# First norm of a hybrid decoder block: the order in which four blocks of rows are loaded, turned and evicted

## The chip, the cores and the metric

The kernel runs on one core of a Trainium2 chip. The core has TensorE (PE, the matrix unit, with its weight loads listed as PEld), VectorE (DVE), ScalarE (ACT), GpSimd (POOL) and SyncE (SP). SP, ACT and POOL can issue DMA transfers, each on a queue of its own. The metric is the device time of one execution in microseconds (us). The profile shows one execution; its span runs from the first to the last instruction.

## The reference

One layer over 512 tokens of width 2048, everything in float32: an RMS norm, one input projection to all branches, a gated short convolution beside a causal attention with a forget bias, a gated merge, an output projection, a second norm, and an MLP with a squared ReLU, then a last norm.

```python
def reference(x, g_mix, w_in, b_f, b_gate, conv_w, w_conv_out, w_attn_out,
              w_mix_out, g_mlp, w_ff1, w_ff2, g_final):
    b, s, _ = x.shape
    for l in range(DEPTH):
        h = rmsnorm(x, g_mix[l])
        z = jnp.einsum('bsd,dc->bsc', h, w_in[l])
        cb, cc, cv, q, k, v, f_logit, gate_c, gate_a = jnp.split(z, SPLIT_POINTS, axis=-1)
        conv_y = cb * causal_dwconv(cc * cv, conv_w[l])
        conv_branch = jnp.einsum('bsc,cd->bsd', conv_y, w_conv_out[l])
        log_f = jax.nn.log_sigmoid(f_logit.astype(jnp.float32) + b_f[l].astype(jnp.float32))
        attn = forgetting_attention(q.reshape(b, s, N_HEADS, HEAD_DIM),
                                    k.reshape(b, s, N_HEADS, HEAD_DIM),
                                    v.reshape(b, s, N_HEADS, HEAD_DIM), log_f)
        attn_branch = jnp.einsum('bsc,cd->bsd', attn, w_attn_out[l])
        gc = jax.nn.sigmoid(gate_c + b_gate[l, :D_MODEL])
        ga = jax.nn.sigmoid(gate_a + b_gate[l, D_MODEL:])
        merged = gc * conv_branch + ga * attn_branch
        x = x + jnp.einsum('bsd,de->bse', merged, w_mix_out[l])
        h = rmsnorm(x, g_mlp[l])
        u = jnp.square(jax.nn.relu(jnp.einsum('bsd,df->bsf', h, w_ff1[l])))
        x = x + jnp.einsum('bsf,fd->bsd', u, w_ff2[l])
    return rmsnorm(x, g_final)
```

What matters here is the beginning: `h = rmsnorm(x, g_mix)`, and the first products of `h` with columns of `w_in` (attention V, K and Q).

## The kernel before

The 512 tokens are four blocks of 128 rows. A block of `x` (128 x 2048, 1 MB) lies in SBUF with tokens on the partitions. The products need it the other way round, with features on the partitions, so the first norm does the following for each block (`Quarters.block`, line 354): four ScalarE squares with running sums (`square_part`, line 327), one small VectorE reduction and a GpSimd power for the reciprocal root (`rstd_of`, line 320), a diagonal matrix `dg` that holds that factor (line 358), then matmuls of the block against `dg` that turn and scale it at once into a PSUM bank, four tiles of 128 x 128 a bank, with banks 6 and 7 in turn (line 362). VectorE evicts each bank in two instructions that also multiply by the gain of the feature (line 367). The profile counts each of these turning matmuls as two records: 32 for a block.

Products are made by a seven-product scheme over 2 x 2 quarters. The activations are cut into token halves (blocks 0 and 1; blocks 2 and 3) and into even and odd tiles of features: quarters A11, A12 for the first token half, A21, A22 for the second, and four sums and differences S1 to S4 of them. Each float32 operand is split into a high part, rounded by a ScalarE copy (line 101), and a low part, which VectorE subtracts out (line 102); each product is then three matmuls, high by high, high by low, low by high. Quarters lie in SBUF as such pairs (`put`, line 351).

A group of columns (class `Group`, line 166) has two column halves of four weight quarters, 1 MB each, which `load` brings in on SP's queue (line 180), into one of four buffers x0 to x3 that a list `free` hands round. Its work is cut in two:

- `head` (line 216) loads two weight quarters, X[0, 0] and X[1, 0], multiplies them by A11 and A12 and adds the two results. It needs blocks 0 and 1 only. Each of the two products is 48 matmuls of 128 x 256; the weights' split goes into `th` and `tl`, two buffers of each.
- `tail` (line 232) makes the other five products with S4, S2, S3, S1 and A22, and needs all four blocks.

The first five groups are one of V (`gV0`, through `mm_rows`, where the first 24 matmuls of a product need only block 0 and the other 24 block 1) and four of K and Q (through `mm_cols`, each matmul needing both blocks). The code runs the five heads, then `Q1.sums()` (line 375: four VectorE sums or differences of 128 x 2048 and four splits), then the five tails.

The code before the heads loads the four blocks on SP's queue, block 0 in four pieces and the others in two (lines 390 to 395), the small rows of gains and biases on ScalarE's queue behind block 0 in the code (lines 397 to 406), then squares and turns block 0, block 1, and then squares of blocks 2 and 3 before both are turned. Blocks 0 and 1 are split into A11 and A12 as soon as each is turned, blocks 2 and 3 into A22 (lines 369 to 373). The rest of the kernel (attention, convolution, gates, merge, MLP) is not touched.

No order of instructions is written out by hand. The framework places each instruction in its engine's queue by its position in the code and by when it takes its inputs to be ready, and it adds the waits. An engine's queue is then worked through in that fixed order. So an instruction that stands later in the code can be queued earlier, and an instruction whose input is late holds up what is queued behind it.

Of the kernel before, what the change touches and what calls it, by code (L numbers as in the profile page):

```python
# [15 lines left out]
P = 128  # L16
# [29 lines left out]
def tile_hybrid_block(ctx: ExitStack, tc, x, g_mix, w_in, b_f, b_gate, conv_w, w_conv_out,  # L46
# [118 lines left out]

    class Group:
# [7 lines left out]
        def load(self, i, j):  # L174

            t = main.tile([P, KT // 2, self.w], F32, tag=f"x{free[0]}", name=f"x{i}{j}")
            self.at[i, j] = free.pop(0)
            c = self.cs[j]
            src = self.view[:, c:c + self.w].rearrange("(q two p) c -> two p q c", two=2, p=P)
            nc.sync.dma_start(out=t, in_=src[i])  # L180
            return t
# [34 lines left out]
        def head(self, keep=False, between=lambda: None):  # L216

            X = self.X = {}
            X[0, 0], X[1, 0] = self.load(0, 0), self.load(1, 0)
# [110 lines left out]
    class Quarters:  # L330
# [23 lines left out]
        def block(self, xt, part, t):  # L354
# [4 lines left out]
            for c in range(4):  # L359
# [6 lines left out]
                for par in range(2):  # L366
                    nc.vector.tensor_tensor(out=self.H[i, par][:, 2 * c:2 * c + 2, ts], in0=p2[:, par],
                                            in1=g2[:, par].unsqueeze(2).to_broadcast([P, 2, P]), op=ALU.mult)
# [3 lines left out]
            else:  # L372
                self.put("A22", self.H[1, 1], ts)
# [14 lines left out]
    xin = []  # L388
    xp = [pair(2 + i, F32, "xn") for i in range(2)]
    for t in range(NT):  # L390
        h = xp[t // 2][:, t % 2]
        n = 4 if t == 0 else 2
        for i in range(n):
            nc.sync.dma_start(out=h[:, i * D // n:(i + 1) * D // n], in_=x[t * P:(t + 1) * P, i * D // n:(i + 1) * D // n])
        xin.append(h)
        if t == 0:
            rows = main.tile([NV, P], F32, tag="x3", name="rows")
            r0 = 0
            for src, n in ((g_mix[0], KT), (g_mlp[0], KT), (b_gate[0], 2 * KT)):
                nc.scalar.dma_start(out=rows[r0:r0 + n, :], in_=src.rearrange("(k p) -> k p", p=P))  # L400
                r0 += n
            nc.scalar.dma_start(out=rows[r0:r0 + 3 * CT, :], in_=conv_w[0].rearrange("j (k p) -> (j k) p", p=P))
            nc.scalar.dma_start(out=bf, in_=b_f.to_broadcast([P, NH]))
            pv = bank(7, "pv")
            nc.tensor.transpose(pv[:, :NV], rows, ident[:NV, :NV])
            nc.vector.tensor_copy(cols, pv[:, :NV])
# [6 lines left out]
    def squares(t):  # L413
        for i in range(4):
            square_part(xin[t][:, i * S:(i + 1) * S], ss1[:, t, i:i + 1], junk[:, i * S:(i + 1) * S])

# [636 lines left out]
```

## Time and profile before

| | |
|---|---|
| median of 3 runs | 2546.12 us (2540.99 to 2546.52) |
| the profiled execution | 2549.66 us |
| its span | 2547.8 us |
| TensorE's mean granted clock | 0.992 |
| TensorE busy | 2469.5 us, 97% of the span |
| TensorE busy in the first 50 us | 37.27 us |
| VectorE busy, first 40 to 60 us and 60 to 80 us | 19.35 and 19.99 of 20 us |
| ScalarE busy in the same stretches | 13.09 and 11.73 of 20 us |
| GpSimd busy in the same stretches | 0.00 and 2.56 of 20 us |

How to read a row of the timelines: start, duration, engine, line of the kernel, operation, what it writes and what it reads, the tile's shape and number of instructions; in brackets how long the engine stood idle before it and what ended that wait. PE's busy time counts matmuls from start to modelled end, so neighbours overlap: what a product takes is read from the starts. A helper's line (101, 102, 105, 108) stands for all its uses, so tiles tell them apart: `xn` are rows of x, `ptr` the turned banks, `h` the evicted quarters, `A` and `S` the split quarters, `x` the weights, `th` and `tl` their split, `a` to `d` the accumulators. A row such as SPq or ACTq is an engine's queue issuing a DMA.

### The profile page before, as it was taken

How to read it: one execution, taken by the hardware profiler on the slowest of the kernel's cores; microseconds unless marked ns; L12 is line 12 of the kernel's file. 1: busy time of each engine (PE TensorE's matmuls, PEld its weight loads, DVE VectorE, ACT ScalarE, POOL GpSimd, SP SyncE). 2: the span in 40 equal slices, each digit the busy share in tenths (PEclk: the TensorE clock that was granted, in tenths of full speed). 3: DMA queues.
4: the chain of work that ended last, by engine and by line, in shares of the span. 5: the costliest groups of instructions: out<-in, count | busy, mean ns of one | idle time of the engine just before them, and what ended most of it. 6: DMA issues, size and time to landing. Idle time of an engine off the chain costs nothing.

```text
span 2547.8 us, 39010 instructions
## 1 busy us (share of the span) xinstructions
PE 2469.5 (97%) x16895; PEld 2269.4 (89%) x16895; DVE 1904.8 (75%) x1498; ACT 1144.5 (45%) x1120; POOL 128.2 (5%) x184
## 2 busy tenths in 40 slices
PE   8999999999999999999989999999999999999997
PEld 7999899999999988888889999999998887787785
DVE  7877677779767734435778888888887878878888
ACT  6433443344444622235545655655654333333343
POOL 0000000000000000000001111111111000000000
PEclk9999999999999999999999999999999999999998
DMA  7554444466443544436565665757587556654573
GB/s 240 158 186 153 155 137 129 133 195 210 138 150 115 199 159 143 136 118 231 167 199 182 216 218 189 246 171 236 193 299 286 181 210 219 226 194 162 191 256 106
DMA packets 287871, 473.45 MB, mean 186 GB/s; under 512 B 10236, under 2 KB 194644, under 8 KB 283476
## 3 DMA queue, kind: packets, MB, share of 16 engines
q1 hardware_dynamic: 260704, 330.40, 40.6%
q0 software_dynamic: 26128, 139.47, 14.7%
q8 instruction: 132, 2.16, 0.3%
q10 hardware_dynamic: 868, 1.10, 0.1%
q14 instruction: 39, 0.32, 0.0%
HBM read 374.46 MB, written 96.47 MB: 185 GB/s over the span
## 4 chain that ended last, share of the span: by engine, by line
PE 49%; DVE 12%; DMA 10%; issue 6%; ACT 4%; POOL 1%; POOLq 0%; ACTq 0%; SPq 0%; DVEq 0%
DMA s_d<-r 5%; DVE tl L102 5%; DMA x<-in_w_ff_dram 4%; ACT th L101 4%; PE a L137 3%; PE a L139 3%; PE a L141 3%; PE a L154 3%; PE a L155 2%; PE a L157 2%; PE pt L295 2%; PE pn L304 2%; PE pn L302 2%; PE pt L297 2%; PE pn L303 2%
## 5 line engine op out<-in xcount | busy, mean ns | idle before, releaser
L102 DVE TENSOR_TENSOR tl<-x,th 128x2048 fp32r<-128x2048 f32 (+1 forms) x252 | 576.0, 2289 | 215.0 <-ACT th L101 199.9
L101 ACT ACTIVATE th<-x 128x2048 fp32r<-128x2048 f32 (+1 forms) x252 | 481.8, 1916 | 474.1 <-PE a L139 164.2
L105 DVE TENSOR_TENSOR x<-x,x 128x2048 f32<-128x2048 f32 (+1 forms) x144 | 329.3, 2287 | 32.5 <-DMA x<-in_w_ff_dram 24.8
L101 ACT ACTIVATE th<-y 128x2048 fp32r<-128x2048 f32 x80 | 153.6, 1921 | 270.2 <-DVE y L105 102.9
L102 DVE TENSOR_TENSOR tl<-y,th 128x2048 fp32r<-128x2048 f32 x80 | 182.8, 2285 | 43.6 <-ACT th L101 43.6
L137 PE MATMUL a<-ST,th 128*128 128x256 f32 x768 | 186.1, 286 | 22.6 <-ACT th L101 19.7
L154 PE MATMUL a<-th,us 128*128 128x512 f32 x512 | 201.7, 394 | 4.4 <-ACT o L836 3.4
L102 DVE TENSOR_TENSOR tl<-raw,th 128x2048 fp32r<-128x2048 f32 x40 | 91.7, 2293 | 150.7 <-ACT th L101 150.2
L155 PE MATMUL a<-th,us 128*128 128x512 f32 x512 | 200.1, 391 | 0.0
L139 PE MATMUL a<-ST,th 128*128 128x256 f32 x768 | 184.4, 283 | 0.0
L137 PEld LDWEIGHTS a<-ST,th 128*128 128x128 f32 x768 | 149.7, 195 | 25.4 <-ACT th L101 22.3
L101 ACT ACTIVATE th<-raw 128x2048 fp32r<-128x2048 f32 x40 | 76.7, 1918 | 176.7 <-PE pt L296 71.5
L139 PEld LDWEIGHTS a<-ST,th 128*128 128x128 f32 x768 | 149.7, 195 | 0.0
L137 PE MATMUL a<-S,th 128*128 128x256 f32 x576 | 136.2, 280 | 4.3 <-ACT th L101 4.2
L157 PE MATMUL a<-tl,us 128*128 128x512 f32 x512 | 136.8, 389 | 0.1
L139 PE MATMUL a<-S,th 128*128 128x256 f32 x576 | 135.6, 279 | 0.0
L154 PEld LDWEIGHTS a<-th,us 128*128 128x128 f32 x512 | 96.6, 189 | 29.6 <-ACT th L101 6.2
L137 PE MATMUL d<-ST,th 128*128 128x256 f32 x512 | 118.1, 277 | 1.0 <-ACT o L194 1.0
L139 PE MATMUL d<-ST,th 128*128 128x256 f32 x512 | 118.0, 276 | 0.0
L155 PEld LDWEIGHTS a<-th,us 128*128 128x128 f32 x512 | 96.7, 189 | 19.7
L157 PEld LDWEIGHTS a<-tl,us 128*128 128x128 f32 x512 | 96.0, 188 | 20.4 <-DVE tl L102 0.5
L137 PEld LDWEIGHTS a<-S,th 128*128 128x128 f32 x576 | 108.5, 188 | 5.6 <-ACT th L101 5.3
(276 smaller groups left out, 6257.8 us busy)
## 6 DMA issues: line engine op xcount, KB each, us to landing
x<-in_w_in_dram SPq DMA_DIRECT2D x86, 1024.0 KB, 5.8
x<-in_w_ff_dram SPq DMA_DIRECT2D x66, 1024.0 KB, 8.4
y<-in_w_ff_dram SPq DMA_DIRECT2D x64, 1024.0 KB, 6.2
us<-s_d POOLq DMA_DIRECT2D x24, 2048.0 KB, 10.0
s_d<-rh POOLq DMA_DIRECT2D x32, 896.0 KB, 6.4
s_d<-r POOLq DMA_DIRECT2D x32, 896.0 KB, 7.8
raw<-in_w_mix_out_dram SPq DMA_DIRECT2D x24, 1024.0 KB, 5.1
g_d<-o SPq DMA_DIRECT2D x32, 256.0 KB, 2.2
```

What stands on the lines that cost most here:

```text
L101: nc.scalar.activation(out=hi, in_=src, func=AF.Copy)
L102: nc.vector.tensor_tensor(out=lo, in0=src, in1=hi.bitcast(F32), op=ALU.subtract)
L105: nc.vector.tensor_tensor(out=out, in0=a, in1=b, op=ALU.subtract)
L137: nc.tensor.matmul(o, hi[:, q, js], Sh, start=first and q == 0 and j == 0, stop=False, skip_group_check=True)
L139: nc.tensor.matmul(o, hi[:, q, js], Sl, start=False, stop=False, skip_group_check=True)
L141: nc.tensor.matmul(o, lo[:, q, js], Sh, start=False, stop=q == nq - 1, skip_group_check=True)
L154: nc.tensor.matmul(o, Sh, hi[:, q, :], start=begin and q == 0, stop=False, skip_group_check=True)
L155: nc.tensor.matmul(o, Sl, hi[:, q, :], start=False, stop=False, skip_group_check=True)
L157: nc.tensor.matmul(o, Sh, lo[:, q, :], start=False, stop=q == nq - 1, skip_group_check=True)
L295: nc.tensor.matmul(ps[j], hi[:, q, js], xh, start=k == 0, stop=False)
L297: nc.tensor.matmul(ps[j], lo[:, q, js], xh, start=False, stop=k == kt - 1)
L302: nc.tensor.matmul(ps, xh, hi, start=first, stop=False)
```

## The change

- A helper `behind(place, done)` has GpSimd copy one column of `done` into the place that a DMA will overwrite, so that this DMA comes after whatever wrote `done`.
- Block 0 comes in two halves on SP's queue and block 1 in two halves on ScalarE's, ahead of the small rows there. Blocks 2 and 3 each come in one DMA on GpSimd's queue, and only after `last_part`, the last column of block 1's low part of A12, is written.
- The first group's first weight load waits for the first element of block 0's evicted quarter, its second weight load for `last_part`.
- Blocks 0 and 1 are squared and turned at the start. Block 2 is squared and turned behind the first head in the code, block 3 behind the second.
- The banks of blocks 2 and 3 are evicted by ScalarE, 16 copies of 128 x 128 a block with the gain as a factor by partition, in place of VectorE's 8 of 128 x 256.
- A22 is split once as a whole (128 x 2048), in place of twice 128 x 1024.

```diff
@@ -163,6 +163,10 @@

     free, later = [0, 1, 2, 3], []

+    def behind(place, done):
+
+        nc.gpsimd.tensor_copy(place, done)
+
     class Group:

 
@@ -171,12 +175,14 @@
             self.view, self.cs, self.w, self.ST, self.mm, self.banks = view, (c1, c2), w, ST, mm, banks
             self.put, self.scale, self.at = put, scale, {}

-        def load(self, i, j):
+        def load(self, i, j, after=None):

             t = main.tile([P, KT // 2, self.w], F32, tag=f"x{free[0]}", name=f"x{i}{j}")
             self.at[i, j] = free.pop(0)
             c = self.cs[j]
             src = self.view[:, c:c + self.w].rearrange("(q two p) c -> two p q c", two=2, p=P)
+            if after is not None:
+                behind(t[:, 0, 0:1], after)
             nc.sync.dma_start(out=t, in_=src[i])
             return t

@@ -213,10 +219,10 @@
         def done(self, *ij):
             free.append(self.at.pop(ij))

-        def head(self, keep=False, between=lambda: None):
+        def head(self, keep=False, between=lambda: None, after=(None, None)):

             X = self.X = {}
-            X[0, 0], X[1, 0] = self.load(0, 0), self.load(1, 0)
+            X[0, 0], X[1, 0] = self.load(0, 0, after[0]), self.load(1, 0, after[1])
             self.a = self.acc("a")
             self.run(self.a, "A11", X[0, 0], True)
             s1 = self.snap(self.a)
@@ -364,13 +370,16 @@
                 p2 = pt.rearrange("p (q two b) -> p two q b", two=2, b=P)
                 g2 = self.gT[:, 4 * c:4 * c + 4].rearrange("p (q two) -> p two q", two=2)
                 for par in range(2):
-                    nc.vector.tensor_tensor(out=self.H[i, par][:, 2 * c:2 * c + 2, ts], in0=p2[:, par],
-                                            in1=g2[:, par].unsqueeze(2).to_broadcast([P, 2, P]), op=ALU.mult)
+                    if i == 0:
+                        nc.vector.tensor_tensor(out=self.H[i, par][:, 2 * c:2 * c + 2, ts], in0=p2[:, par],
+                                                in1=g2[:, par].unsqueeze(2).to_broadcast([P, 2, P]), op=ALU.mult)
+                        continue
+                    for q in range(2):
+                        nc.scalar.activation(out=self.H[i, par][:, 2 * c + q, ts], in_=p2[:, par, q], func=AF.Copy,
+                                             scale=g2[:, par, q:q + 1])
             if i == 0:
                 self.put("A11", self.H[0, 0], ts)
                 self.put("A12", self.H[0, 1], ts)
-            else:
-                self.put("A22", self.H[1, 1], ts)

         def sums(self):
             H = self.H
@@ -385,43 +394,39 @@

     ph = ExitStack()
     px = ph.enter_context(phase("px"))
-    xin = []
     xp = [pair(2 + i, F32, "xn") for i in range(2)]
-    for t in range(NT):
-        h = xp[t // 2][:, t % 2]
-        n = 4 if t == 0 else 2
+    xin = [xp[t // 2][:, t % 2] for t in range(NT)]
+
+    def load_x(t, n, queue=nc.sync):
         for i in range(n):
-            nc.sync.dma_start(out=h[:, i * D // n:(i + 1) * D // n], in_=x[t * P:(t + 1) * P, i * D // n:(i + 1) * D // n])
-        xin.append(h)
-        if t == 0:
-            rows = main.tile([NV, P], F32, tag="x3", name="rows")
-            r0 = 0
-            for src, n in ((g_mix[0], KT), (g_mlp[0], KT), (b_gate[0], 2 * KT)):
-                nc.scalar.dma_start(out=rows[r0:r0 + n, :], in_=src.rearrange("(k p) -> k p", p=P))
-                r0 += n
-            nc.scalar.dma_start(out=rows[r0:r0 + 3 * CT, :], in_=conv_w[0].rearrange("j (k p) -> (j k) p", p=P))
-            nc.scalar.dma_start(out=bf, in_=b_f.to_broadcast([P, NH]))
-            pv = bank(7, "pv")
-            nc.tensor.transpose(pv[:, :NV], rows, ident[:NV, :NV])
-            nc.vector.tensor_copy(cols, pv[:, :NV])
+            cs = slice(i * D // n, (i + 1) * D // n)
+            queue.dma_start(out=xin[t][:, cs], in_=x[t * P:(t + 1) * P, cs])
+
+    load_x(0, 2)
+    load_x(1, 2, nc.scalar)
+    rows = main.tile([NV, P], F32, tag="x3", name="rows")
+    r0 = 0
+    for src, n in ((g_mix[0], KT), (g_mlp[0], KT), (b_gate[0], 2 * KT)):
+        nc.scalar.dma_start(out=rows[r0:r0 + n, :], in_=src.rearrange("(k p) -> k p", p=P))
+        r0 += n
+    nc.scalar.dma_start(out=rows[r0:r0 + 3 * CT, :], in_=conv_w[0].rearrange("j (k p) -> (j k) p", p=P))
+    nc.scalar.dma_start(out=bf, in_=b_f.to_broadcast([P, NH]))
+    pv = bank(7, "pv")
+    nc.tensor.transpose(pv[:, :NV], rows, ident[:NV, :NV])
+    nc.vector.tensor_copy(cols, pv[:, :NV])
     ss1 = const.tile([P, NT, 5], F32, name="ss1")
     nc.vector.memset(ss1[:, :, 4:5], EPS)
     Q1 = Quarters(px, gmixT)

     junk = pair(6, F32, "junk")[:, 1]

-    def squares(t):
+    def norm_block(t):
         for i in range(4):
             square_part(xin[t][:, i * S:(i + 1) * S], ss1[:, t, i:i + 1], junk[:, i * S:(i + 1) * S])
-
-    for t in (0, 1):
-        squares(t)
         Q1.block(xin[t], ss1[:, t, :], t)
-    for t in (2, 3):
-        squares(t)
-    Q1.tiles("A22")
-    for t in (2, 3):
-        Q1.block(xin[t], ss1[:, t, :], t)
+
+    norm_block(0)
+    norm_block(1)

 
     def store_v(c0, w):
@@ -453,7 +458,17 @@
         g.tail()

     heads = [gV0] + [kq(hp, ((a,), (3,), (6,), (7,))) for hp, a in enumerate((0, 1, 2, 5))]
-    for g in heads:
+    last_part = Q1.ST["A12"][:, 1, KT // 2 - 1, HS - 1:].bitcast(F32)
+    for t in (2, 3):
+        behind(xin[t][:, 0:1], last_part)
+        load_x(t, 1, nc.gpsimd)
+    heads[0].head(after=(Q1.H[0, 0][:, 0, 0:1], last_part))
+    norm_block(2)
+    heads[1].head()
+    norm_block(3)
+    Q1.tiles("A22")
+    Q1.put("A22", Q1.H[1, 1])
+    for g in heads[2:]:
         g.head()
     Q1.sums()
     ph.close()
```

## The prediction

> **What bounds the kernel now.** I read the page first, then the busy time by stretches of the first 140 us, then the timelines of each engine there, and the waits last. The page says that TensorE is the bound over the whole span:
>
> ```profile
> PE 2469.5 (97%) x16895; PEld 2269.4 (89%) x16895; DVE 1904.8 (75%) x1498; ACT 1144.5 (45%) x1120; POOL 128.2 (5%) x184
> PE   8999999999999999999989999999999999999997
> ```
>
> So an edit in the first 100 us is worth what it moves the moment at which TensorE has finished the five heads, plus the holes it makes behind that. The stretches show where TensorE is not yet at work, and what clock it has (columns: span, busy us of PE, PEld, DVE, ACT, POOL, granted clock, DMA share, GB/s):
>
> ```profile
> 4.00:6.00 2.00, 0.00 (x0) 0.00 (x0) 0.00 (x0) 1.52 (x5) 0.00 (x0) 1.00 1.01 375
> 22.00:24.00 2.00, 0.58 (x5) 0.61 (x6) 2.00 (x5) 1.67 (x1) 0.00 (x0) 1.00 1.09 347
> 24.00:26.00 2.00, 2.00 (x14) 2.00 (x14) 0.95 (x4) 0.95 (x1) 0.55 (x1) 0.67 1.10 350
> 26.00:28.00 2.00, 2.00 (x12) 2.00 (x11) 1.94 (x4) 2.00 (x3) 0.00 (x0) 0.50 0.83 267
> ```
>
> From 24 us on it does not stop, but at 24 to 28 us it runs at 0.67 and 0.50 of its clock, right behind a stretch in which it was idle. The timelines of VectorE and TensorE give the chain:
>
> ```profile
> 13.59 0.16 DVE L322 TENSOR_REDUCE v<-ss 128x1 f32<-128x5 f32 x1 [4.80 <-ACT junk L328]
> 13.67 0.76 DVE L367 TENSOR_TENSOR h<-ptr,cols 128x256 f32<-128x256 f32 x2
> 26.73 2.35 DVE L102 TENSOR_TENSOR A<-h,A 128x1024 fp32r<-128x1024 f32 x2
> 45.27 2.28 DVE L108 TENSOR_TENSOR h<-h,h 128x2048 f32<-128x2048 f32 x1
> 80.43 2.29 DVE L105 TENSOR_TENSOR x<-x,x 128x2048 f32<-128x2048 f32 x1 [0.15 <-DMA x<-in_w_in_dram]
> 82.64 2.07 DVE L514 COPY sel<-identb 8x1024 bf16<-8x1024 bf16 x3
> 85.61 2.29 DVE L105 TENSOR_TENSOR x<-x,x 128x2048 f32<-128x2048 f32 x1 [0.90 <-DMA x<-in_w_in_dram]
> ```
>
> ```profile
> 25.68 0.56 PE L154 MATMUL a<-th,A 128*128 128x256 f32 x1
> 86.18 1.98 PE L141 MATMUL b<-A,tl 128*128 128x256 f32 x16
> ```
>
> See four things. VectorE stands 4.80 us behind block 1's reduction while block 0's first turned bank waits. The first two blocks' A12 is whole at 29.08 us. The first weight matmul is at 25.68, the last of the heads ends at 88.16. And VectorE has only 3.1 us of slack between the sums and the first tail: 0.15 and 0.90 idle, and 2.07 of copies that nobody needs yet.
>
> **The change, part by part.** TensorE's work from the first weight matmul on is fixed: first head 96 matmuls at 0.118 us (11.3), four heads of 10.90 (44.46 to 55.36), blocks 2 and 3's 64 transpose records at 1.95 us for 16 (7.8): 62.7 us. The heads end that long after the start, plus holes.
>
> *Rows of blocks 0 and 1, 2.1 MB together on SP's and ScalarE's queues.* The stretches move 0.45 MB at 2 to 4 us and 0.75 at 4 to 6; the rest at 375 GB/s ends at 8.4. Block 0 is 1.9 us later than now (its last quarter is squared from 6.55), block 1 is 3.8 earlier (12.22). ScalarE issues two more DMAs (about 0.45 each) before the five small loads, which then queue behind 1 MB: they land near 9.3 instead of 6.2 us. The gains are first needed by an eviction at 13, so 3.7 us cover it; without this each us late is a us of the start.
>
> *Block 0 and block 1.* Four squares at 0.66 each; block 0's end at 9.7, block 1's at 12.3. Square end to transposes is 1.3 us now (7.27 to 8.56), so TensorE starts at 11.0. 16 records take 3.78 us, the other 16 some 3.0 as it comes to speed: 17.8. The 4.80 us wait is gone, since block 1's reduction is ready at 12.4, before the first bank. Its last eviction (0.68 a bank) ends at 18.5, the hi splits (2.0) at 20.5, the lo splits at 21.7. Block 1: four evictions 2.7 and block 0's lo splits 2.35 share VectorE: 23.4, hi to 25.4, lo to 26.7. That is 2.4 us before today's 29.08.
>
> *First weights, held until block 0's first eviction.* Eviction near 13.5, a one-column copy on GpSimd (0.10, from its 128x1 memset), then 5.2 to 5.3 us to landing as for the loads of an empty queue at 32.69 and 36.16: 19.0. The split (1.9) stands behind block 0's hi splits: 22.4. So the first weight matmul is at 22.4 instead of 25.68; its first half lasts 2.8, the second needs block 1's A11 at 25.6, a hole of 0.4. End of the heads 22.4 + 0.4 + 62.7 = 85.5 against 88.16: **-2.7 us**. Bounds: -5.5 if block 0's splits end 2.4 us sooner and the hole goes, 0 if the rows land 2.7 us later.
>
> *Second weights, held until block 1 is split.* SP's queue now stands on a wait until 26.7 us, and whatever is behind it too. GpSimd first makes two copies and issues two row loads (0.73 each in the row of L656), so the copy for the weights is at 28.4 and the load at 28.6. Alone it lands at 33.8, split at 35.7. Until then TensorE has the first product of head 0 (to 28.5) and, if its weights are already in their free buffers, that of head 1 (to 33.9). SP's queue does not follow the program: these rows show the store of head 0, which stands before head 2's loads in the code, issued behind them:
>
> ```profile
> 8.66 35.34 SPq L180 DMA_DIRECT2D x<-in_w_in_dram  x7
> 45.38 0.37 SPq L431 DMA_DIRECT2D v_d<-o  x1
> ```
>
> So I take head 1's loads as sent early. The hole is between 0 (head 1's second product goes ahead) and 4.6 us (the load shares the engines with 2.1 MB of rows: 3 us more at 350 GB/s). I take **+2.5**, nearer the shared case, because 11.6 to 14.1 us is what these loads take today with others queued. The Trainium skill says in "DMA: Bandwidth & Descriptors", section "Queues, rings and completion order", that each DMA engine goes round the queues that have work, a packet at a time; this stage of the trace has no load on GpSimd's queue, so it neither agrees nor differs. By that rule the hole is 4.6 and the sum 2.1 us higher.
>
> *Blocks 2 and 3.* They land at about 34 and 37 us (4.1 to 7.8 us from issue in the row of L656, plus sharing). Their 8 squares (5.2 us) and the new evictions move onto ScalarE in 30 to 55 us. An eviction of 128x256 with a column factor (L717) follows the next by 0.36, so 32 of 128x128 cost between 5.8 and 11.4; I take 0.26 each, 8.3. VectorE loses 16 x 0.34 = 5.4. ScalarE is busy 15.3 of 30 us at 30 to 60 now and gets 13.5 more: no cover is left there, block 3 ends near 50 and A22's whole split (1.9 + 2.2, instead of two halves) near 54. So the first sum on VectorE moves from 45.27 to about 54. That is 34.0 us before the end of the heads (85.5 + 2.5 = 88.0) instead of 42.9. Of the 8.9 us of lead lost, 8.9 / 5.45 = 1.6 products of the heads are by then done, which takes 1.6 x 2.5 = 4.1 us of splits and sums off VectorE's rest; 3.1 is slack; 1.7 shows as a hole before the first tail's S2. **+1.7**; bounds 0 (sums by 51) and 5 (sums at 57).
>
> *The copies and the wider A22 split* cost nothing else: GpSimd is idle from 24.70 to 77.44 us. Were it not, every load behind a copy would come later by as much.
>
> Sum: -2.7 + 2.5 + 1.7 = **+1.5 us**. The profiled execution took 2549.66 us (span 2547.8 and 1.9 around it), 3.5 above the median of the three runs, 2546.12; so 2551.2 under the profiler and **2547.6** beside that median. 0.2%, 5.1 us, is about what a measurement of this kernel tells from no change.
>
> **The rivals.** *Both held loads are hidden (22 in 100).* Head 1's two products run while the second weights arrive, no hole, sums by 51; with the better front, -5.5: 2540.6 us. For it: SP's queue above, and four matmul runs' worth of weights fit the four buffers. Against it: it needs each of three estimates at its good end.
>
> *TensorE stands behind blocks 2 and 3's transposes (30 in 100).* Engines take instructions in a fixed order: VectorE's 4.80 us stall is exactly such a case, a reduction put ahead of an eviction that was ready. If block 2's transposes stand ahead of weights that are ready and its rows land after 30 us (33.9 less squares 2.6 and chain 1.3; the point from which it decides), TensorE waits at 33.9 until 39.6 for rows that land at 35.7: 5.7 instead of 2.5. The clock then drops: behind the idle stretch at 22 us, 2 us at 0.67 and 2 at 0.50 lost 1.7. Sum -2.7 + 5.7 + 1.7 + 1.7 = +6.4: 2552.5 us. "TensorE: Matmul & The Clock Gate" of the Trainium skill, "Part 1: The HAM clock gate", gives half clock after an idle window of about 3.4 us; the trace's drop stands behind a shorter hole, of some 2.3 us, so the row speaks more strongly.
>
> *Head 1's weights are not sent early (8 in 100).* If SP's order has them behind the second weights, TensorE has nothing from 28.5 to 35.7: 7.2, then the clock's 1.7: -2.7 + 7.2 + 1.7 + 1.7 = +7.9: 2554.0 us. Against it: the two SP rows.
>
> **How the numbers follow.** My forecast, the two holes eating the earlier start, has 40 in 100, by itself 2543 to 2551. Faster 0.22 (hidden loads), same 0.40, slower 0.38 (30 and 8). The range takes the hidden case with a us beyond (2539.5) and the last rival with 2 (2556).
>
> **What would show it.** Right: rows of both blocks squared without a gap by 12 to 13 us and no wait of VectorE on block 1's reduction; first weight matmul at 21 to 23; end of the heads at 86 to 89; a TensorE gap of 1 to 4 us near 34; the first sum at 51 to 57. Wrong: if head 0's second product starts before 33 us, if no gap over 1 us is there and the first tail starts by 84, it is the first rival; a gap over 5 us with clock 0.5 behind it is the second; an SP queue whose second weight load comes before head 1's is the third. If the ends of the heads differ by 3 us but the whole by more than 6, the rest of the kernel took another order and my sum misses its cause.

## The result and the profile after

The changed kernel took 2579.2 us (median of 4 runs, 2565.17 to 2580.46) against 2546.3 us (2540.99 to 2548.36) for the kernel before: a ratio of 1.0118, 95% interval 1.0094 to 1.0141. It is slower by 33 us by the medians, by 30 us by the ratio. The prediction was 2547.6 us with 2556 as its upper end, so it was wrong in size by far, and its likeliest case (no change) was wrong too. The profiled execution took 2580.46 us (span 2578.8), 30.8 us more than the one shown of before.

The page after. In the line of slices TensorE's first slice (64 us) falls from 8 to 5 tenths and its second from 9 to 8; the rest is as before:

```profile
PE 2487.9 (96%) x16895; PEld 2288.0 (89%) x16895; DVE 1900.0 (74%) x1481; ACT 1154.5 (45%) x1151; POOL 132.2 (5%) x190
PE   5899999999999999999989999999999999999997
```

The stretches of after, the four of before and two more (columns: span, busy us of PE, PEld, DVE, ACT, POOL, granted clock, DMA share, GB/s):

```profile
4.00:6.00 2.00, 0.00 (x0) 0.00 (x0) 0.00 (x0) 0.00 (x0) 0.00 (x0) 1.00 0.82 223
22.00:24.00 2.00, 1.85 (x16) 1.60 (x14) 2.00 (x4) 2.00 (x3) 0.00 (x0) 1.00 0.00 0
24.00:26.00 2.00, 0.90 (x6) 0.75 (x7) 2.00 (x5) 1.05 (x1) 0.00 (x0) 1.00 0.00 0
26.00:28.00 2.00, 2.00 (x20) 2.00 (x19) 2.00 (x2) 0.00 (x0) 0.00 (x0) 1.00 0.00 0
40.00:42.00 2.00, 0.00 (x0) 0.00 (x0) 0.00 (x0) 0.00 (x0) 0.00 (x0) 0.50 1.03 426
48.00:50.00 2.00, 2.00 (x11) 2.00 (x11) 1.01 (x3) 2.00 (x4) 0.56 (x1) 0.50 0.14 30
```

From 22 to 28 us nothing is being loaded at all (0 GB/s, against 267 to 350 before), and at 40 to 42 us loads are all that happens: no engine computes. TensorE's timeline after has these five landmarks, each with the idle time ahead of it in brackets, and its last product of the heads:

```profile
25.10 0.39 PE L154 MATMUL a<-th,A 128*128 128x256 f32 x1 [1.25 <-ACT th L101]
31.15 0.39 PE L155 MATMUL a<-th,A 128*128 128x256 f32 x1 [0.88 <-DVE A L102]
46.29 0.58 PE L154 MATMUL b<-th,A 128*128 128x256 f32 x1 [12.16 <-ACT th L101]
103.32 1.98 PE L141 MATMUL b<-A,tl 128*128 128x256 f32 x16
107.95 0.39 PE L154 MATMUL c<-th,S 128*128 128x256 f32 x1 [2.66 <-ACT th L101]
119.55 0.58 PE L154 MATMUL a<-th,S 128*128 128x256 f32 x1 [3.86 <-ACT th L101]
```

Read downwards: the first weight matmul is hardly earlier than before (25.10 against 25.68); head 0's second product waits 12.16 us; the heads end at 105.30 instead of 88.16; the first tail's S4 product (`c`) and its S2 product (`a<-th,S`) then wait again, so that S2 starts at 119.55 instead of 94.99, 24.6 us late. Counted along TensorE's timelines, the 600th weight matmul is 27.3 us late; so most of the 30.8 us is lost by then, in the first 130 us.

VectorE after, the rows that answer to those of before (the first eviction, block 1's reduction, block 1's low part of A12, the first sum). Block 1's reduction now runs without a wait:

```profile
16.38 0.76 DVE L374 TENSOR_TENSOR h<-ptr,cols 128x256 f32<-128x256 f32 x2 [2.17 <-PE ptr L368]
17.05 0.15 DVE L328 TENSOR_REDUCE v<-ss 128x1 f32<-128x5 f32 x1
29.87 2.36 DVE L102 TENSOR_TENSOR A<-h,A 128x1024 fp32r<-128x1024 f32 x2 [0.80 <-ACT A L101]
80.67 2.29 DVE L108 TENSOR_TENSOR h<-h,h 128x2048 f32<-128x2048 f32 x1
```

A12 is whole at 32.23 (before 29.08), and the first sum comes at 80.67 (before 45.27). ScalarE's timeline shows a late start and what the long hole waits for:

```profile
7.69 0.54 ACTq L412 DMA_DIRECT2D rows<-in_conv_w_dram  x1
8.68 0.63 ACT L334 ACTIVATE junk<-xn 128x512 f32<-128x512 f32 x1 [5.92 <-DMA rows<-in_conv_w_dram]
44.33 1.91 ACT L101 ACTIVATE th<-x 128x2048 fp32r<-128x2048 f32 x1 [9.57 <-DMA x<-in_w_in_dram]
```

The fourth small load is issued at 7.69 us (2.20 before), and the first square, behind it in the same queue, at 8.68 (4.32 before). The chain of work that ended last in the first 30 us (start, duration, what) tells how that reaches TensorE:

```profile
0.81 6.86 DMA xn<-in_x_dram
7.69 4.74 DMA rows<-in_conv_w_dram
12.94 0.04 DVE cols L416
13.11 0.16 DVE v L328
14.26 7.58 PE ptr L368 x40
```

The fourth small load is issued only when a load of rows, issued at 0.81 us, has landed. The copy of the gains (`cols`) waits for that small load, and in VectorE's order block 0's reduction (`v`) stands behind the copy; in the kernel before the reduction came first (7.30, the copy at 8.56). The late first square matters less: the third one starts at 10.08, just when its half of block 0 has landed (issued at 1.25, 8.8 us).

The split of the second weights waits for their load; the view of DMA issues between 30 and 46 us (size of one, median us from issue to landing) gives that load and the two rows beside it:

```profile
xn<-in_x_dram POOLq DMA_DIRECT2D x2, 1024.0 KB, 9.8
x<-in_w_in_dram SPq DMA_DIRECT2D x1, 1024.0 KB, 11.5
```

### The profile page after: what moved, and what is told of

It reads as the page before. It is cut to its first block, busy times and chain, and to the rows that moved or that the text cites. A ratio compares the mean times of both kernels' runs of the same rounds, so it can differ in the third digit from the quotient of the medians.

```text
span 2578.8 us, 39011 instructions
## 1 busy us (share of the span) xinstructions
PE 2487.9 (96%) x16895; PEld 2288.0 (89%) x16895; DVE 1900.0 (74%) x1481; ACT 1154.5 (45%) x1151; POOL 132.2 (5%) x190
## 4 chain that ended last, share of the span: by engine, by line
PE 63%; DVE 13%; DMA 12%; issue 6%; ACT 5%; POOL 1%; SPq 0%; POOLq 0%; ACTq 0%; DVEq 0%
DMA s_d<-r 6%; DVE tl L102 5%; ACT th L101 4%; PE a L141 4%; PE a L137 4%; PE a L139 4%; PE a L154 3%; PE a L155 3%; PE a L157 3%; DMA x<-in_w_ff_dram 3%; PE d L137 3%; PE d L139 3%; PE d L141 2%; PE d L157 2%; PE pt L301 2%
## 6 DMA issues: line engine op xcount, KB each, us to landing
us<-s_d POOLq DMA_DIRECT2D x24, 2048.0 KB, 10.1
```

## The experiments

Two remarks on reading the times. One execution wanders by some 10 us either way (20 runs of before beside the first four experiments: 2535.3 to 2557.45), so the ratios resolve some 5 to 8 us, and finer steps are read from the first 130 us of the traces, where most positions are set by waits. There too the pace of the matmuls differs (last section): a later head of 96 matmuls takes 10.88 us in some traces and 11.30 in others (second weights free, block 1 on SP, VectorE evicts, turned behind the heads, hold alone, turned ahead), which is 1.7 us of a heads' end over four heads. For three kernels the ratio fell by more than the trace accounts for: from the changed kernel by 21 us of 2546 with the second weights free, 14 with the rows behind the weights and 12 with block 1 on SP, where S2 comes 14.1, 5.9 and 4.7 us earlier; the changed kernel's own ratio rests on four executions. "Late work" below is the time from the heads' end to the first tail's S2 product, "lead" the time from the first sum to the heads' end; both are worked out from rows of each trace.

| kernel | ratio to before | idle ahead of head 0's second product | heads' end | first sum | lead | S2 starts | late work |
|---|---|---|---|---|---|---|---|
| before | 1 | none | 88.16 | 45.27 | 42.9 | 94.99 | 6.8 |
| after | 1.0118 [1.0094, 1.0141] | 12.16 | 105.30 | 80.67 | 24.6 | 119.55 | 14.3 |
| second weights free | 1.0034 [1.0005, 1.0063] | none | 92.43 | 66.55 | 25.9 | 105.43 | 13.0 |
| block 1 on SP | 1.0069 [1.0045, 1.0093] | 12.73 | 101.85 | 75.96 | 25.9 | 114.84 | 13.0 |
| rows behind weights | 1.0062 [1.0030, 1.0093] | 7.14 | 99.41 | 74.78 | 24.6 | 113.66 | 14.3 |
| VectorE evicts | 1.0100 [1.0068, 1.0131] | 12.37 | 106.82 | 82.21 | 24.6 | 121.08 | 14.3 |
| rows early | 1.0053 [1.0035, 1.0071] | none | 96.99 | 72.36 | 24.6 | 111.24 | 14.3 |
| rows early, block 1 on SP | 1.0029 [1.0003, 1.0055] | none | 90.01 | 65.38 | 24.6 | 104.25 | 14.2 |
| before, turned behind the heads | 1.0014 [0.9989, 1.0039] | none | 87.22 | 58.59 | 28.6 | 99.55 | 12.3 |
| before, hold alone | 1.0003 [0.9976, 1.0030] | none | 89.71 | 43.38 | 46.3 | 96.91 | 7.2 |
| free, turned ahead | 1.0039 [1.0017, 1.0061] | none | 93.32 | 64.72 | 28.6 | 105.68 | 12.4 |
| head 1 between | 1.0102 [1.0074, 1.0130] | 5.80 | 102.01 | 77.38 | 24.6 | 116.26 | 14.3 |
| before, first weights ahead | 1.0013 [0.9992, 1.0035] | none | 85.50 | 46.54 | 39.0 | 94.29 | 8.8 |
| before, both weights ahead | 1.0004 [0.9982, 1.0027] | none | 84.57 | 44.44 | 40.1 | 92.45 | 7.9 |

### The hold on the second weights

The changed kernel without that hold:

```diff
-    heads[0].head(after=(Q1.H[0, 0][:, 0, 0:1], last_part))
+    heads[0].head(after=(Q1.H[0, 0][:, 0, 0:1], None))
```

> The changed kernel, but the first group's second weight load waits for nothing; the first load keeps its wait, the rows of blocks 2 and 3 stay held. Theory H (the hold on the second weights makes the loss): the 12.2 us TensorE hole at 34 us goes, the five heads end near 93 instead of 105.3, and the time falls by about 12 us, to 2564 to 2570. Rival S (late rows of blocks 2 and 3 make the loss: what the heads win is lost again before the first tail's S2 product, which stands at 119.55 us in the changed kernel): the heads end earlier, but the S2 product still starts after 115 us and the time falls by less than 5 us.

The long hole is gone, the heads end 12.9 us earlier and S2 starts 14.1 us earlier than in the changed kernel; the ratio falls by 0.0084, which is 21 us of 2546. The hold is the largest single part of the loss. What stays is the late work, in these two rows of TensorE's timeline:

```profile
93.84 0.39 PE L154 MATMUL c<-th,S 128*128 128x256 f32 x1 [1.41 <-ACT th L101]
105.43 0.58 PE L154 MATMUL a<-th,S 128*128 128x256 f32 x1 [4.15 <-ACT th L101]
```

The hold alone, put into the kernel before:

```diff
-            X[0, 0], X[1, 0] = self.load(0, 0), self.load(1, 0)
+            X[0, 0], X[1, 0] = self.load(0, 0), self.load(1, 0, after)
...
+    last_part = Q1.ST["A12"][:, 1, KT // 2 - 1, HS - 1:].bitcast(F32)
+    heads[0].head(after=last_part)
```

> The kernel before with the other part alone: the first group's second weight load waits, through a one-column GpSimd copy, for the last column of block 1's low part of A12. Theory H: the copy is at 29 us, the load lands at 35 to 38 with nothing on GpSimd's queue, the split ends 2 us later, TensorE has a hole of 3 to 6 us before head 0's second product, and the time rises by 3 to 8 us. Rival (the hold is harmless without the rows on GpSimd's queue beside it): hole under 1.5 us, time within 2 us.

No change that can be told; the heads' end and S2 are 1.6 and 1.9 us later, about what the slower pace of this trace gives. No rows come beside the held load there, and it lands after 5.3 us (first fence, the view of DMA issues at 28 to 32 us). And TensorE turns blocks 2 and 3 while it waits (second fence, its timeline), so head 0's second product follows without a gap:

```profile
x<-in_w_in_dram SPq DMA_DIRECT2D x1, 1024.0 KB, 5.3
```

```profile
33.04 1.95 PE L364 MATMUL ptr<-dg,xn 128*128 128x128 f32 x16
36.12 1.05 PE L364 MATMUL ptr<-dg,xn 128*128 128x128 f32 x8
38.67 0.28 PE L154 MATMUL b<-th,A 128*128 128x256 f32 x1
```

So the hold by itself costs next to nothing; the change makes it dear by taking away what ran in its shadow and by sending 2 MB of rows beside it.

How much is the sharing? The rows put behind the weights on SP's queue:

```diff
+    heads[0].head(after=(Q1.H[0, 0][:, 0, 0:1], last_part))
     for t in (2, 3):
         behind(xin[t][:, 0:1], last_part)
-        load_x(t, 1, nc.gpsimd)
-    heads[0].head(after=(Q1.H[0, 0][:, 0, 0:1], last_part))
+        load_x(t, 1, nc.sync)
```

> The changed kernel, but the held rows of blocks 2 and 3 go on SP's queue behind the second weights, not on GpSimd's beside them. Theory C (the second weights share the DMA engines with 2 MB of rows): they land 5 to 6 us after issue instead of 11.5, the hole at 34 us shrinks from 12.2 to 6 or 7 us, the time falls by 4 to 6 us. Rival S (late blocks 2 and 3): the rows land no earlier than 43 us, the S2 product of the first tail starts within 2 us of 119.55, the time stays within 2 us.

The load of the second weights now lands after 6.7 us, and the hole is 5.0 us shorter (DMA issues, then TensorE's timeline):

```profile
x<-in_w_in_dram SPq DMA_DIRECT2D x1, 1024.0 KB, 6.7
```

```profile
40.56 0.58 PE L154 MATMUL b<-th,A 128*128 128x256 f32 x1 [7.14 <-ACT th L101]
```

Sharing cost 4.8 us of landing and 5.0 of the hole; the other 7.1 are the load and its split with nothing else ahead of the waiting product in TensorE's queue.

And why did head 1's first product not fill it, as the prediction had it? Its place in the queues, or missing weights? The changed kernel with that product written between head 0's two (`head` is cut into `head_a` and `head_b` for it):

```diff
...
-    heads[0].head(after=(Q1.H[0, 0][:, 0, 0:1], last_part))
+    heads[0].head_a((Q1.H[0, 0][:, 0, 0:1], last_part))
+    heads[1].head_a()
+    heads[0].head_b()
     norm_block(2)
-    heads[1].head()
+    heads[1].head_b()
```

> This is the changed kernel with one difference: head 1's first product (its weights land at 17 to 20 us) is written between the two products of head 0, so that its split and its matmuls stand ahead of the second weights in the queues, as my prediction took them to. Theory (the fixed order of the queues, and not missing data, keeps it out of the hole): TensorE runs 48 matmuls of it behind head 0's first product, from about 34 to 39.7 us, the idle time before head 0's second product falls from 12.2 to 6 to 8 us, the heads end at 98 to 101 us instead of 105.3, the start of the first tail's S2 product comes earlier by about as much, and the time is 2568 to 2575 us. Rival (head 1's weights are not there, or the buffers of the split are not free before the second weights are through): the hole stays at 11 us or more, heads' end at 104 us or later, 2576 us or more. Neither expects it to come near the kernel before.

The idle time halves to 5.80 us, as the theory has it, and TensorE is busy where it had stood. ScalarE's timeline shows both weights split at 22.98 to 26.67 us, so head 1's were there long before the hole; then its split of the second weights, and TensorE's row:

```profile
22.98 3.69 ACT L101 ACTIVATE th<-x 128x2048 fp32r<-128x2048 f32 x2
46.05 1.91 ACT L101 ACTIVATE th<-x 128x2048 fp32r<-128x2048 f32 x1 [2.19 <-DMA x<-in_w_in_dram]
```

```profile
48.02 0.58 PE L154 MATMUL b<-th,A 128*128 128x256 f32 x1 [5.80 <-ACT th L101]
```

The gain at the heads' end is only 3.3 us, less than expected: the A12 wait ahead of the hold is 1.2 us longer (2.07 against 0.88) and the second weights are split 1.7 us later. In the ratio it cannot be told from the changed kernel.

### When blocks 2 and 3 are turned

Two theories for the late work: the rows come late, or their squares and turning stand late in the code. Rows released 15 us earlier, the second weights free:

```diff
     for t in (2, 3):
-        behind(xin[t][:, 0:1], last_part)
+        behind(xin[t][:, 0:1], Q1.H[0, 0][:, 0, 0:1])
...
-    heads[0].head(after=(Q1.H[0, 0][:, 0, 0:1], last_part))
+    heads[0].head(after=(Q1.H[0, 0][:, 0, 0:1], None))
```

> The changed kernel with the second weight load free (as in the first experiment) and the rows of blocks 2 and 3 released by block 0's first eviction (17 us) instead of by block 1's last split (33 us). Theory L (with that hold gone, what is left of the loss is that blocks 2 and 3 come late: the first of VectorE's sums starts at 66.55 us, 26 us before the end of the heads, where the kernel before has 43): the rows land by 28 us, the first sum starts by 56, the holes before the first tail's S2 product (1.41, 1.24 and 4.15 us) fall to under 3 us together, and the time falls by 4 to 9 us, to 2552 to 2557. Rival P (the place of the turning in the code is what is late, not the rows): the first sum stays after 62 us and the time within 3 us of the first experiment's 2560.6.

Early rows did not help: the lead is 24.6 us and the late work 14.3, and the rows now crowd the first weights: these land 11.9 us after their issue (5.4 in the changed kernel), and the first weight matmul waits 4.32 us for their split and starts at 32.10. The same with block 1 on SP's queue as well:

> The same, and block 1's halves on SP's queue. Theory Q (ScalarE standing behind its own DMA issues costs 4 us of the start): first weight matmul near 21 instead of 25.4 us, heads end by 88.5, first sum by 52, and the time is 3 to 5 us under the run before this one, within 5 us of the kernel before. Rival (rows that are released earlier now share the DMA engines with the first weights, which then bound the start): first weight matmul after 24 us, no gain over the run before this one.

Heads' end 90.01, 7.0 us earlier than without that second edit, and the late work unchanged at 14.2. But the first weight matmul comes at 27.07 and not near 21, as the rival had it, and the first sum at 65.38 and not by 52. TensorE stands for 4.66 us ahead of block 2's first turning matmul, which is what the second rival of the prediction had feared for the changed kernel:

```profile
25.36 2.05 PE L368 MATMUL ptr<-dg,xn 128*128 128x128 f32 x8 [4.66 <-DVE dg L364]
```

Next the kernel before, with nothing but the place in the code changed:

```diff
-    for t in (2, 3):
-        squares(t)
-    Q1.tiles("A22")
-    for t in (2, 3):
-        Q1.block(xin[t], ss1[:, t, :], t)
...
-    for g in heads:
+    heads[0].head()
+    for t in (2, 3):
+        squares(t)
+    Q1.tiles("A22")
+    Q1.block(xin[2], ss1[:, 2, :], 2)
+    heads[1].head()
+    Q1.block(xin[3], ss1[:, 3, :], 3)
+    for g in heads[2:]:
         g.head()
```

> The kernel before with one part of the change alone: blocks 2 and 3 are turned behind the first and the second head in the code; loads, queues and VectorE's evictions stay. Theory L: the rows are there by 20 us, so the first sum moves by less than 6 us from 45.27 and the time stays within 4 us of the kernel before. Rival P (the place in the code is what is late): the first sum moves past 55 us, holes of over 3 us stand before the S2 product, the time rises by 5 us or more.

The place alone takes 14.3 us off the lead and adds 5.5 to the late work; S2 starts 4.6 us late, though the ratio does not resolve it. A row of VectorE and one of TensorE:

```profile
58.59 2.29 DVE L108 TENSOR_TENSOR h<-h,h 128x2048 f32<-128x2048 f32 x1
```

```profile
99.55 0.58 PE L154 MATMUL a<-th,S 128*128 128x256 f32 x1 [4.15 <-ACT th L101]
```

Then the converse: turned ahead of the heads in the code, rows still late, the second weights free:

```diff
-    heads[0].head(after=(Q1.H[0, 0][:, 0, 0:1], None))
     norm_block(2)
-    heads[1].head()
     norm_block(3)
     Q1.tiles("A22")
     Q1.put("A22", Q1.H[1, 1])
-    for g in heads[2:]:
+    heads[0].head(after=(Q1.H[0, 0][:, 0, 0:1], None))
+    for g in heads[1:]:
         g.head()
```

> This is the changed kernel with its second weight load not held, and with blocks 2 and 3 squared, turned and split into A22 ahead of the heads in the code, as in the kernel before; their rows are still held until block 1 is split and land near 42 us. Theory P (the place in the code sets when the two blocks are turned): the first VectorE sum comes from 66.5 to 54 to 60 us, the holes ahead of the first tail's S2 shrink from 6.8 us to 2 or less, and the time falls by 4 us or more, to about 2554 to 2557 us. Rival L (the late rows set it): sum and holes as without this edit, 2560 us. Rival S (the squares and transposes now stand ahead of the heads' splits in fixed queues and wait for rows that land at 42 us): a hole of 3 us or more before 45 us, heads' end later than 95 us, time 2562 us or more.

My theory fell here: the first sum is only 1.8 us earlier (64.72) and S2 starts where it did (105.68 against 105.43). A late place with early rows (the kernel before, turned behind the heads) and late rows with an early place (this one) give the same lead of 28.6 us; only where both are early is it kept, as in the kernels "weights ahead" below (39.0 and 40.1).

Which of the two binds can be read from block 3's diagonal (VectorE) and its first turning matmul (TensorE). In the changed kernel:

```profile
53.80 0.28 DVE L364 TENSOR_SCALAR dg<-ident,r 128x128 f32<-128x128 f32 x1 [0.66 <-POOL r L330]
68.62 1.95 PE L368 MATMUL ptr<-dg,xn 128*128 128x128 f32 x16
```

The diagonal is ready 14.5 us before TensorE turns the block, since that matmul stands behind both products of head 1. With rows early the two start at 41.65 and 60.31, in the kernel before turned behind the heads at 33.94 and 49.47: the place binds. With the second weights free they start at 53.13 and 54.50, and turned ahead at 52.82 and 53.21: there the diagonal itself is late, and the place has little left to give. So neither edit helped alone.

The table says more. In the eight kernels with a lead of 24.6 to 25.9 us, S2 starts 38.9 us after the first sum (119.55 - 80.67 in the changed kernel, 105.43 - 66.55 with the second weights free, 104.25 - 65.38 with early rows and block 1 on SP). From the first sum on VectorE is then the bound, with sums, splits and differences of 2.2 us each. The stretch of the changed kernel from the first sum to the end of the last difference ahead of S2 has VectorE (the third busy time of the row) at work for 35.68 of 36.80 us; with the second weights free and with rows early it is 35.68 of 36.80 as well:

```profile
80.67:117.47 36.80, 32.23 (x266) 31.54 (x264) 35.68 (x20) 16.34 (x10) 5.99 (x4) 0.95 0.45 136
```

Who evicts is the remaining part of that edit:

```diff
-                    if i == 0:
+                    if True:
                         nc.vector.tensor_tensor(out=self.H[i, par][:, 2 * c:2 * c + 2, ts], in0=p2[:, par],
```

> The changed kernel, but VectorE evicts blocks 2 and 3 as it does blocks 0 and 1. Theory H (holds and order make the loss, not the evictions): VectorE is idle 14 us before the hole's end and 4.8 at 58 us, so it takes them in; the time stays within 3 us. Rival E (32 small ScalarE copies, 4.4 us for each block, hold up the weights' splits): the splits come earlier, the A22 split starts at 70 instead of 74 us, the time falls by 4 to 8 us.

First sum and S2 are both 1.5 us later with VectorE, which the slower pace of that trace can account for; the lead is the same 24.6 us, and the ratio is not told apart. ScalarE's evictions neither caused the loss nor repaired it.

### The start

Block 1's two halves taken off ScalarE's queue:

```diff
     load_x(0, 2)
-    load_x(1, 2, nc.scalar)
+    load_x(1, 2)
```

> The changed kernel, but block 1's two halves go on SP's queue behind block 0's, so that ScalarE issues only the five small loads. Theory Q (ScalarE's first square stands behind its own DMA issues, which wait until 7.69 us): squares start near 5 instead of 8.68 us, the first turning matmul near 10 instead of 14.26, the first weight matmul near 21 instead of 25.10, the second weights are released 4 us earlier, and the time falls by 3 to 5 us. Rival R (the rows' bytes bound the start): squares start below 7 but the last of block 1 stays at 13 to 14 us, the weights' release moves by less than 1.5 us and the time by less than 2.

The fourth small load goes out at 2.20 us, the squares start at 5.14, and the first weight matmul comes 3.95 us earlier than in the changed kernel (ScalarE's timeline, then TensorE's):

```profile
2.20 0.64 ACTq L412 DMA_DIRECT2D rows<-in_conv_w_dram  x1
5.14 0.63 ACT L334 ACTIVATE junk<-xn 128x512 f32<-128x512 f32 x1 [2.37 <-DMA xn<-in_x_dram]
```

```profile
21.15 0.38 PE L154 MATMUL a<-th,A 128*128 128x256 f32 x1 [0.37 <-ACT th L101]
40.66 0.58 PE L154 MATMUL b<-th,A 128*128 128x256 f32 x1 [12.73 <-ACT th L101]
```

So the better start that the prediction counted on exists, and two row loads on ScalarE's queue took it away. Three things went with that one edit: block 0's second half lands 5.2 us after its issue (8.8 in the changed kernel), no small load waits for rows, and block 0's reduction (7.82) stands ahead of the copy of the gains (9.08) again. How much each is worth was not tested. The hole stays; 3.45 us arrive at the heads' end, in a trace of the slower pace.

The good half of the change by itself, in the kernel before: all rows on SP in halves, the first weight load (then both) ahead of blocks 2 and 3, nothing held, nothing turned later:

```diff
...
+    load_x(0)
+    load_x(1)
...
+    first = [heads[0].load(i, 0) for i in range(1)]
+    load_x(2)
+    load_x(3)
```

> This is the kernel before with one part of the change alone, in another form: every block of rows comes in two halves, all on SP's queue, and the first group's first weight load stands there ahead of blocks 2 and 3 (nothing waits, nothing is turned later, VectorE evicts). My theory of the front (with no DMA issues on ScalarE's queue ahead of the squares, the first weights and not the rows set the start): first weight matmul at 20 to 22.5 us instead of 25.7, heads' end 84.5 to 87 us instead of 88.2, first sum no later than 48 us, time 2 to 4 us under before's, 2542 to 2545 us, which a measurement can hardly tell from no change. Rival (blocks 2 and 3, 1 MB later, hold the second half up as they stand in the fixed queues): first weight matmul early but a hole of 2 us or more behind it, heads' end at 88 us or later, no gain.

> As the kernel with the first weight load ahead of blocks 2 and 3, but with both weight loads of the first group ahead of them. If the second weights set the start of head 0's second product: that product starts at 27 to 29 us, heads' end 83 to 86 us, 2541 to 2544 us. If instead the squares of blocks 2 and 3 stand ahead of the splits of block 1 or of the weights in ScalarE's fixed queue, their rows, 2 MB later, stop it: a ScalarE wait of 2 us or more on those rows between 20 and 30 us, heads' end at 88 us or later, and a time of 2548 us or more.

With one load ahead TensorE's first weight matmul comes at 17.2 us (then it waits 1.99 us for A11's low part), the heads end at 85.50 and S2 starts 0.7 us earlier than before. With both, head 0's second product starts at 24.62, the heads end at 84.57 and S2 starts at 92.45, 2.5 us earlier:

```profile
20.02 0.39 PE L155 MATMUL a<-th,A 128*128 128x256 f32 x1 [1.99 <-DVE A L102]
92.45 0.38 PE L154 MATMUL a<-th,S 128*128 128x256 f32 x1 [0.79 <-ACT th L101]
```

The heads' ends came out as expected and the first products earlier still (17.2 for an expected 20 to 22.5, 24.62 for 27 to 29); the times did not follow: 2548.09 and 2547.16 us beside 2545.57 for before, both within what can be told from no change. No version here is shown to beat the kernel before.

## Why the prediction was wrong

By its own steps, from its starts and ends (said: heads' end 85.5 + 2.5, then 6.8 + 1.7 to S2, 96.5):

| step | said, us | measured, us | more |
|---|---|---|---|
| first weight matmul | at 22.4 | at 25.10 | 2.7 |
| head 0's first product | 6.1, to 28.5 | 9.0, to 34.1 | 2.9 |
| hole before its second | 2.5 | 12.16 | 9.7 |
| from there to the heads' end | 57.0 | 59.0 | 2.0 |
| heads' end to S2 | 8.5 | 14.25 | 5.7 |
| S2 starts | 96.5 | 119.55 | 23.0 |

- **Rows of blocks 0 and 1: the bytes and the small loads failed.** The text had all rows landed by 8.4 us and the small loads 3 us late, first needed by an eviction, "so 3.7 us cover it". Block 0's second half lands at 10.1 us: 1 MB of weights, which SP issues at 1.72 us, comes beside the 2.1 MB that the text counted, and 223 GB/s were moved at 4 to 6 us where the sum took 375. Block 0's squares end at 11.42 (said 9.7). And the first to need the small loads is not an eviction but the copy of the gains, ahead of block 0's reduction in VectorE's order: the reduction runs at 13.11, 1.7 us behind the squares, and the transposes start at 14.26 (said 11.0). That an issue is an instruction in ScalarE's queue and held the first square for 5.92 us added little to that, since the third square starts as its data lands. Without the two loads there, the first weight matmul comes at 21.15, better than the 22.4 said. Why the small load's issue waits for a load of rows stays open.
- **Block 1: what ends head 0's first product.** Right that VectorE's 4.80 us wait would go. But A12 is whole at 32.23, not 26.7; 3.3 us of that is the late start, the evictions wait for TensorE's banks (2.17, 0.89, 0.76 us), which the sum had as back to back, and block 1's last bank, turned by 26.83, is evicted at 28.33, behind the weights' low part on VectorE (2.28 us), which the sum did not have there.
- **Second weights: "TensorE has ... that of head 1 (to 33.9)" is the step that failed most.** The text let head 1's first product run in the hole, took 2.5 us for what was left, and the hole was 12.16. SP did send head 1's weights early, as the text read from SP's rows, and in the test they were split long before. But loaded weights are not queued work: in ScalarE's and TensorE's fixed order head 1's split (48.59) and matmuls stood behind the second weights' (44.33). The reordered kernel took 6.4 us off the hole. The landing was mis-sized too: "3 us more at 350 GB/s" is what 1.05 MB take, half of the 2.1 MB beside the load; all of them take 6.0 us, and 6.2 more were measured (11.5 against 5.3). The rule of "DMA: Bandwidth & Descriptors" ("Queues, rings and completion order") of the Trainium skill, that the engines go round the queues with work, agrees in so far as both queues were served beside each other: the two rows and the weights, issued together, land after 9.8 (median) and 11.5 us. An equal share by bytes, which the 3 us stand for, is not what the rows show. And the load went out at 32.7, not 28.6, since block 1 was late.
- **No clock loss in the sum.** After the hole the clock is 0.50 to about 50 us; head 0's second product takes 7.8 us instead of 5.6 as the others do. That is the 2.0. The second and third rival had priced such a loss (1.7), the forecast had not.
- **Blocks 2 and 3: the method held, its input did not.** The text turned a lost lead of 8.9 us into +1.7. The measured loss of lead is 42.9 - 24.6 = 18.3; the same sum (18.3 / 5.45 products of 2.5 us off, 3.1 slack off) gives 18.3 - 8.4 - 3.1 = 6.8, and 7.4 was measured (14.25 - 6.83). With the second weights free it gives 6.1 for 6.2. What failed is the "first sum near 54": it came at 80.67, behind the hole and behind block 3, which is turned from 68.62 on, 14.5 us after its diagonal is ready, because its matmuls stand behind head 1's.
- **The rivals.** The second had the right kind (a fixed order, then the clock) with the wrong blocker: it was not block 2's transposes, but the held weights. The third had the right picture (nothing from head 0's first product to its second) with the wrong cause. By the sign that the text set for it (a gap over 5 us with clock 0.5 behind it) the trace would be the second, so that sign does not tell the two blockers apart. Both were priced with a hold that ends at 26.7 and a load that shares half of what it did, so the worst came out at +8 us.
- **Nothing lost from the evictions**, as the text had it: the new engine for them is worth at most 1.5 us.

Of the 30.8 us between the two profiled executions these steps hold 24.6 by S2 (23.0 and the 1.5 that was forecast), and 2.7 more fall until the 600th weight matmul, where S2 itself runs at half clock behind the 3.86 us hole. The last 3.5 us, over 2450 us of the same work, are within what one run differs from the next.

## What to carry to other kernels

A hold on a load costs the landing less the work that the waiting engine still has queued ahead of the wait; data that merely lies in the buffers does not count. So list what stands ahead of the wait in each engine's order, and charge the whole landing, with every load that is released by the same event, if the list is empty. A load put ahead of small ones on a queue delays them too: follow the smallest to whatever stands behind it in any engine's order (here a reduction behind the copy of the gains). When work is moved later, find the engine that has to go on from it (here VectorE, 38.9 us from the first sum to S2) and count back from when its result is needed.

## What was not expected of the hardware

Matmuls of 128 x 256 run at two speeds at the same granted clock. The same stretch of the kernel before, the changed one and "both weights ahead":

```profile
600.00:700.00 100.00, 99.89 (x858) 99.69 (x857) 77.46 (x50) 48.35 (x51) 0.10 (x1) 1.00 0.54 170
```

```profile
600.00:700.00 100.00, 100.00 (x851) 100.00 (x850) 84.83 (x62) 48.53 (x46) 0.30 (x3) 1.00 0.55 176
```

```profile
600.00:700.00 100.00, 99.57 (x879) 99.37 (x878) 80.87 (x52) 50.63 (x53) 0.10 (x1) 1.00 0.50 159
```

With TensorE busy throughout and a clock of 1.00, 851 and 858 matmuls in 100 us (0.1175 and 0.1166 us each) against 879 (0.1138), 3% more. "Head 1 between" also has 879 there; its profiled run took 2555.23 us although S2 starts at 116.26, its other five runs 2561.98 to 2571.38. Both speeds occur within one execution too: in the kernel before a later head's 96 matmuls take 10.88 us (0.1133 each), and the stretch at 600 to 700 us has 0.1166. The later heads of the changed kernel have 0.1133, those with the second weights free 0.1177 (11.30 us). That this makes the times wander by 10 us is likely and not shown. What chooses the speed stays open; no run tried it.

A short hole can be enough to halve the clock: behind the 2.66 us ahead of `c`, the stretches of the changed kernel give 0.65 at 108 to 110 us and 0.50 at 110 to 112. "TensorE: Matmul & The Clock Gate" of the Trainium skill ("Part 1: The HAM clock gate") names a free-running window of about 3.4 us; the hole measured here is shorter than that, and the row decides. It is not always so: with rows early the hole ahead of `c` is 2.66 us as well, and the clock stays at 1.00 in both stretches from 100 to 104 us. What tells the two cases apart was not tested.
